# A two-layer decoder trunk on one core: three pairs of projection slabs of the sparse mixer as seven block products, and a new order of its begin

## The chip, the core and the metric

The kernel runs on one core of a Trainium2 chip. TensorE (PE in the profile, PEld for its weight loads) multiplies and writes to PSUM, which has eight banks; VectorE (DVE), ScalarE (ACT) and GpSimd (POOL) do the elementwise work, and transfers are issued from SyncE's queue (SP) and from ACT's. Each engine works through its own list of instructions in order and waits at semaphores for the others. The metric is the device time of one execution in microseconds (us).

## What is computed

A trunk of two layers over 512 tokens of width 1024, in float32. Each layer is a half-weighted SwiGLU network, a token mixer and a second half-weighted SwiGLU network, each behind an RMS norm. Layer 0 mixes with latent attention, layer 1 with native sparse attention. The change lies in the begin of the latter:

```python
def nsa_mixer(h, rel_bias, w_in, pos_k, w1_k, w2_k, pos_v, w1_v, w2_v, w_o):
    ...
    q, k_c, v_c, k_s, v_s, k_w, v_w, g = jnp.split(h @ w_in, cuts, axis=-1)
    ...
    gates = jax.nn.sigmoid(g.astype(jnp.float32)).astype(h.dtype).reshape(B, S, G, R, 3)
    ...
    kc = compress_blocks(k_c, blk_idx, pos_k, w1_k, w2_k)
    vc = compress_blocks(v_c, blk_idx, pos_v, w1_v, w2_v)
    ...
    o = gates[..., 0:1] * o_cmp + gates[..., 1:2] * o_sel + gates[..., 2:3] * o_win
    return o.reshape(B, S, H * NSA_V) @ w_o
```

Here h is the normed input (512 x 1024), q holds 16 heads of 64, and every k and v holds 4 groups of 64.

## The kernel before

**Numbers.** Every float32 factor is split in two parts of TensorE's faster format, high and low: ACT copies (rounding to the high part), DVE subtracts. A product is then three matmuls: high x high, high x low, low x high (`mm3`, L166 to L168, and `product`, L361 to L363). A weight slab is 128 columns of a projection, 1024 x 128, held as a tile of 128 x 1024; `wslab` loads it into one of two raw buffers (tile wr), and ACT and DVE split it into one of three tiles w (L147, L149). While the attention runs, POOL does the subtraction instead (L153).

**Block products.** A network's gate and up slab are two outputs of the same input. Their two halves of the weights' rows and the two halves of the tokens make a 2 x 2 by 2 x 2 block product, which the kernel forms with seven products of 12 matmuls of 256 columns in place of eight (`ffn`, L492 to L504). For this it needs sums of blocks: of the input (`combine`, L236 to L244: tiles y, u, and the split into a tile four) and of the weights (`wsums`, L346 to L353: tile s1, sums in place in the two raw tiles, three splits of 128 x 1024 and one of 128 x 512). Results come out in tiles px, pq and pg in PSUM, with copies on ACT and two additions on DVE.

**The sparse mixer's begin** (`nsa`, L1078 to L1117) uses plain slabs, 24 matmuls of 512 columns each (`proj`, and `pieces` in quarters). In the program's order: two slabs of compression keys (`tokens`, PSUM tile pcm); the norm's factors (`norm_col`: sums pc by TensorE, a chain of twelve small DVE instructions on tile small; `norm_bcast`: tile pb, copied to row); their layout into xc (`layout`, DVE, 8 instructions); two slabs of compression values; the compression network (`hidden`, tile ph, 16 matmuls); the keys of group 0 (`keys(0)`, PSUM tile pp, then t and four parts); the layout of the values; `pkc`; the second `hidden`; two query slabs (`query(0)`, `query(1)`); the values and gates (tiles pvg, 96 matmuls of 304 columns; `values` then splits them in alternation on ACT and DVE, and ACT forms the sigmoid gat); and `pvc`. 

**The attention behind it** runs in tiles (`attend`): scores on TensorE (L1180, L1205), softmax on DVE, ACT and POOL, transposes and the product with the values on TensorE. Into it `make` hands pieces of later projections by tile numbers, in group 1 the keys of group 1 at tiles 11 to 19. 

**What sets the order.** The order of the instructions on each engine is set before the run by a scheduler that interleaves the program's parts by its own estimates; the program gives the tiles and their buffers. PSUM's banks go by tags: two of mm, two of S, three of T, one of o. `mm_bank` turns through the first three kinds; `bank` takes the one that is named. A tile whose buffers are all in use waits until the oldest is read.

Of the kernel before, what the change touches and what calls it, by code (L numbers as in the profile page):

```python
# [11 lines left out]
F32 = mybir.dt.float32  # L12
# [33 lines left out]
FGAINS = "a0", "b0", "a1", "b1"  # L46
LASTK = 4
# [17 lines left out]
class Kern:  # L65
# [13 lines left out]
    def setup(self):  # L79
        nc, cp, a = self.nc, self.cp, self.a  # L80

        self.nw, self.odd, self.nq = 0, 0, 0
        self.first = self.wp.tile([P, 2048 + 3 * PAD], F32R, tag="w0", name="w")
        small = self.wp.tile([P, 80], F32, name="small")
        self.vtc, self.small_sums, self.stc = small[:, :12], small[:, 12:16], small[:, 32:]
        self.sts, self.nst = [small[:, 12 + 4 * i : 16 + 4 * i] for i in range(5)], 0
        self.gains = cp.tile([P, 64], F32, name="gains")
        nc.scalar.dma_start(self.gains[:, :53], a["gains"])  # L90
        self.ident = cp.tile([P, P], F32, name="ident")
        nc.scalar.dma_start(self.ident, a["c_ident"])
# [7 lines left out]
        self.ngains = cp.tile([P, 32], F32, name="ngains")  # L100
        for i, x in enumerate(FGAINS):
# [125 lines left out]
    def combine(self, p):  # L227


        nc, fp = self.nc, self.fp  # L230
        y = fp.tile([P, 1024], F32, tag="fh", bufs=3, name="y")
        u = fp.tile([P, 1024 + 2 * PAD], F32, tag="fl", bufs=3, name="u")[:, :1024]
        for e in range(2):
            c = p + KP * e
            with self.tc.issue_after(self.weights.ins) if self.weights else nullcontext():
                nc.scalar.activation(y[:, e * S : e * S + S], self.h[c], AF.Copy, scale=self.gains[:, self.ng + c : self.ng + c + 1])  # L236
# [6 lines left out]
        t = self.four()  # L243
# [57 lines left out]
    def proj(self, src, m, xh, xl, name, w=None):  # L301
# [3 lines left out]
        p = self.mm_bank(name)  # L305
# [50 lines left out]
    def product(self, j, w, out, first, last):  # L356
        mm = self.nc.tensor.matmul
        wh, wl = w[j]
        for p in range(KP):
# [3 lines left out]
            mm(out, wl[:, p], xh, start=False, stop=last and p == KP - 1, skip_group_check=True)  # L363

# [566 lines left out]
    def nsa(self, gain_next):  # L931
        nc, tc, a = self.nc, self.tc, self.a
        with ExitStack() as cx:
# [13 lines left out]
            xh, xl = self.xh, self.xl  # L947
            kt = [self.four() for _ in range(2)]
            kp = self.parts(kt[0]) + self.parts(kt[1])
            pcp, self.qt = self.parts(self.four()), self.parts(self.four())  # L950
# [18 lines left out]
            def keys(g):  # L969
# [3 lines left out]
                def done(p):  # L973
                    tt.append(qp.tile([P, S], F32, tag="t", bufs=2, name="t"))
                    nc.vector.tensor_tensor(tt[0], p, row, op=ALU.mult)
# [11 lines left out]
                return pieces(a["nsa_w_k"][g], done, [partial(part, br) for br in range(2)])  # L987
# [29 lines left out]
            def query(t2):  # L1017
# [3 lines left out]
                def done(p):  # L1021
                    tt.append(qp.tile([P, S], F32, tag="t", bufs=2, name="t"))
                    nc.vector.scalar_tensor_tensor(tt[0], p, 0.125, row, op0=ALU.mult, op1=ALU.mult)
# [8 lines left out]
                return pieces(a["nsa_w_q"][t2], done, [partial(part, e) for e in range(2)])  # L1032
# [3 lines left out]
            with tc.tile_pool(name="cmp", bufs=1, reuse_waits="tile") as bp:  # L1036
# [5 lines left out]
                def tokens(kind):  # L1042
                    return [self.proj(a["nsa_w_c"][2 * kind + gp], P, xh, xl, "pcm") for gp in range(2)]

                def layout(kind, ps):
# [6 lines left out]
                    for gp, p in enumerate(ps):  # L1052
                        for e in range(2):
                            g = 2 * gp + e
                            for odd in range(2):
                                src, rs = [t[64 * e : 64 * e + 64, :].rearrange("p (n l o) -> p n l o", l=8, o=2)[:, :, :, odd] for t in (p, row)]
                                dst = xc[64 * odd : 64 * odd + 64, :, 32 * g : 32 * g + 32].rearrange("p l n -> p n l")
                                nc.vector.tensor_tensor(dst, src, rs, op=ALU.mult)
# [19 lines left out]
                ps = tokens(0)  # L1078
                col = self.norm_col(D, self.s2)
                nc.scalar.activation(row, self.norm_bcast(col), AF.Copy)  # L1080
# [4 lines left out]
                for f in kf[:3]:  # L1085
                    f()
                xc = layout(1, ps)
                pk = self.mm_bank("pkc")
                nc.tensor.matmul(pk[:, : G * 32], w2, hid.rearrange("p g n -> p (g n)"), start=True, stop=True)
                at = lambda t: t[:, 96:].rearrange("p (g n) -> p g n", g=G)[:, :, 0:32]  # L1090
                self.split(pk[:, : G * 32].rearrange("p (g n) -> p g n", g=G), at(kch), at(kcl))
                for f in kf[3:]:
                    f()
                hid, w2 = hidden(1, xc)
                for f in query(0) + query(1):
                    f()

                pv = [self.mm_bank("pvg") for _ in range(4)]
# [7 lines left out]

                pk = self.mm_bank("pvc")
# [6 lines left out]
                for j in range(4):  # L1114
                    values(0, j, pv[j])
                    nc.scalar.activation(gat[:, j, :], pv[j][:, 256:VG], AF.Sigmoid, scale=col[:, j : j + 1])
                nc.vector.tensor_tensor(gcmp, gat[:, :, 0 : 3 * H : 3], rvalid[:, :, None].to_broadcast([P, 4, H]), op=ALU.mult)  # L1117
# [319 lines left out]
```

## Time and profile before

| | |
|---|---|
| median of 3 runs (lowest, highest) | 1864.89 us (1862.98, 1866.41) |
| span of the profiled execution, first to last instruction | 1860.0 us |
| mean granted TensorE clock | 0.999 |
| the sparse mixer's begin (first pcm matmul to the first scores) | 1216.9 to 1280.0 us |

For the profiled execution only the span is given; the median of the runs stands 4.9 us above it. A row of a timeline shows start, duration, engine, line, operation, the tile written and the tiles read, and shapes. TensorE's matmuls overlap: their durations are modelled ends, so what a matmul takes of the engine is read from the distance between two starts.

### The profile page before, as it was taken

To read this page: it belongs to the slowest core of one execution; us is meant where nothing else is said; L and a number is where in the kernel's file an instruction comes from. 1 tells how busy PE (TensorE), PEld (TensorE's weight loads), DVE (VectorE), ACT (ScalarE), POOL (GpSimd) and SP (SyncE) were. 2 spreads that over 40 slices of the span, in tenths; PEclk is the share of its full clock that TensorE was granted. 3 is DMA by queue.
4 is the path that set the end of the run, shared out by engine and by line. 5 is a ranking of instruction groups with operands and counts; after the bars stand their busy time and mean duration, and the time that the engine had idled before them with its cause. 6 is when DMAs were issued, how large, how long until landed. Compare 5 with 4: busy or idle time off the path is not lost. (4 is left out here: it accounts for less than half of the span.)

```text
span 1860.0 us, 32734 instructions
## 1 busy us (share of the span) xinstructions
PE 1841.1 (99%) x12440; PEld 1679.9 (90%) x12440; DVE 1542.0 (83%) x2862; ACT 1083.9 (58%) x2044; POOL 232.9 (13%) x323
## 2 busy tenths in 40 slices
PE   8999999999999999999999999999999999999998
PEld 8999999888889999998999999888888889999997
DVE  8988886688789888887998888765988989988885
ACT  8545554479776554555654545435887866544554
POOL 0000000046500000000000000015666600000000
PEclk9999999999999999999999999999999999999999
DMA  6333333142342333323233332333221124333321
GB/s 245 130 103 102 103 97 115 49 106 72 94 134 94 103 105 112 112 88 115 91 116 110 103 107 87 96 100 97 63 74 63 44 104 131 107 103 106 102 80 67
DMA packets 77901, 187.44 MB, mean 101 GB/s; under 512 B 9632, under 2 KB 37664, under 8 KB 77744
## 3 DMA queue, kind: packets, MB, share of 16 engines
q1 hardware_dynamic: 74640, 180.32, 30.3%
q10 hardware_dynamic: 3104, 5.03, 0.8%
q8 instruction: 98, 1.61, 0.3%
q14 instruction: 59, 0.48, 0.1%
HBM read 178.17 MB, written 2.16 MB: 97 GB/s over the span
## 5 line engine op out<-in xcount | busy, mean ns | idle before, releaser
L167 PE MATMUL pd<-al,wd 128*128 128x512 f32 x576 | 224.1, 389 | 0.0
L168 PE MATMUL pd<-ah,wd 128*128 128x512 f32 x576 | 224.0, 389 | 0.0
L166 PE MATMUL pd<-ah,wd 128*128 128x512 f32 x576 | 224.0, 389 | 0.0
L361 PE MATMUL px<-four,wh 128*128 128x256 f32 x632 | 175.2, 277 | 0.5 <-ACT pg L493 0.5
L363 PE MATMUL px<-four,wl 128*128 128x256 f32 x632 | 174.5, 276 | 0.0
L362 PE MATMUL px<-four,wh 128*128 128x256 f32 x632 | 174.5, 276 | 0.0
L362 PE MATMUL pq<-four,wh 128*128 128x256 f32 x632 | 174.5, 276 | 0.0
L363 PE MATMUL pq<-four,wl 128*128 128x256 f32 x632 | 174.4, 276 | 0.0
L361 PE MATMUL pq<-four,wh 128*128 128x256 f32 x632 | 174.4, 276 | 0.0
L174 ACT ACTIVATE wd<-wdr 128x384 fp32r<-128x384 f32 x192 | 99.2, 519 | 101.5 <-issue 75.5
L175 DVE TENSOR_TENSOR wl<-s,wh 128x512 fp32r<-128x512 f32 x79 | 54.6, 691 | 121.0 <-ACT wh L174 120.9
L413 DVE SCALAR_TENSOR_TENSOR h<-pd,h 128x512 f32<-128x512 f32 x216 | 148.5, 688 | 6.1 <-PE pd L168 6.1
L174 ACT ACTIVATE wh<-s 128x512 fp32r<-128x512 f32 x79 | 49.8, 630 | 136.5 <-PE px L362 131.2
L168 PEld LDWEIGHTS pd<-ah,wd 128*128 128x128 f32 x576 | 108.2, 188 | 22.5
L166 PEld LDWEIGHTS pd<-ah,wd 128*128 128x128 f32 x576 | 108.1, 188 | 19.4
L167 PEld LDWEIGHTS pd<-al,wd 128*128 128x128 f32 x576 | 108.0, 188 | 19.5
L361 PEld LDWEIGHTS px<-four,wh 128*128 128x128 f32 x632 | 118.6, 188 | 1.6 <-ACT pg L493 1.3
L362 PEld LDWEIGHTS px<-four,wh 128*128 128x128 f32 x632 | 118.6, 188 | 0.0
L363 PEld LDWEIGHTS pq<-four,wl 128*128 128x128 f32 x632 | 118.6, 188 | 0.0
L363 PEld LDWEIGHTS px<-four,wl 128*128 128x128 f32 x632 | 118.6, 188 | 0.0
L362 PEld LDWEIGHTS pq<-four,wh 128*128 128x128 f32 x632 | 118.6, 188 | 0.0
L361 PEld LDWEIGHTS pq<-four,wh 128*128 128x128 f32 x632 | 118.6, 188 | 0.0
(367 smaller groups left out, 6037.5 us busy)
## 6 DMA issues: line engine op xcount, KB each, us to landing
wr<-in_w_gu SPq DMA_DIRECT2D x93, 512.0 KB, 3.2
ru<-in_w_gu SPq DMA_DIRECT2D x79, 512.0 KB, 4.2
wdr<-in_w_down SPq DMA_DIRECT2D x192, 192.0 KB, 2.5
wdr<-in_w_down SPq DMA_DIRECT2D x24, 256.0 KB, 2.9
wr<-in_mla_w_o SPq DMA_DIRECT2D x8, 512.0 KB, 3.5
wr<-in_nsa_w_q SPq DMA_DIRECT2D x8, 512.0 KB, 3.5
th<-btab_d SPq DMA_DIRECT2D x16, 256.0 KB, 3.3
wr<-in_nsa_w_o SPq DMA_DIRECT2D x8, 512.0 KB, 3.6
```

Source lines behind the costliest of these rows:

```text
L166: mm(out, wh, xh, start=first, stop=False)
L167: mm(out, wh, xl, start=False, stop=False)
L168: return mm(out, wl, xh, start=False, stop=last)
L174: nc.scalar.activation(hi, src, AF.Copy)
L175: (nc.gpsimd if pool else nc.vector).tensor_tensor(lo, src, f32v(hi), op=ALU.subtract)
L361: mm(out, wh[:, p], xh, start=first and p == 0, stop=False, skip_group_check=True)
L362: mm(out, wh[:, p], xl, start=False, stop=False, skip_group_check=True)
L363: mm(out, wl[:, p], xh, start=False, stop=last and p == KP - 1, skip_group_check=True)
L413: nc.vector.scalar_tensor_tensor(self.h[c], p, 0.5, self.h[c], op0=ALU.mult, op1=ALU.add)
```

## The change

Three pairs of slabs go from 2 x 24 matmuls of 512 columns to seven products of 256: the compression values (`nsa_w_c[2:4]`), the keys of groups 0 and 1 (`nsa_w_k[0:2]`) and the queries of the first two pairs of heads (`nsa_w_q[0:2]`). The keys of group 1 leave the attention for this. The block sums of the input are formed with the negated gain (a new entry in ngains), so some results come with the other sign, which the following multiplication by row takes back. The values and gates move forward, behind the first pair, which stays plain.

```diff
+    def combos(self, p, y, u, t, gains, at):
+        ...
+                nc.scalar.activation(y[:, e * S : e * S + S], self.h[c], AF.Copy, scale=gains[:, at + c : at + c + 1])
...
+    def seven(self, w, uq, t):
+
+        nc = self.nc
+        x, q, g = self.bank("S", "px")[:, :HS], self.bank("mm", "pq")[:, :HS], self.bank("T", "pg")
+        self.product(1, w, x, True, False)
+        nc.scalar.activation(g[:, :HS], x, AF.Copy)
+        self.product(7, w, q, True, False)
+        nc.scalar.activation(uq[:, :HS], q, AF.Copy)
+        self.product(6, w, x, False, False)
+        nc.scalar.activation(uq[:, HS:], x, AF.Copy)
+        self.product(2, w, g[:, :HS], False, True)
+        self.product(5, w, x, False, True)
+        nc.scalar.activation(g[:, HS:], x, AF.Copy)
+        nc.vector.tensor_tensor(t[:, HS:], x, uq[:, :HS], op=ALU.add)
+        self.product(4, w, q, False, True)
+        nc.vector.tensor_tensor(t[:, :HS], q, uq[:, HS:], op=ALU.add)
+        self.product(3, w, g[:, HS:], False, True)
+        return g
...
-                def tokens(kind):
-                    return [self.proj(a["nsa_w_c"][2 * kind + gp], P, xh, xl, "pcm") for gp in range(2)]
+                def both(src):
+
+                    rg, ru = [self.wp.tile([P, 1024], F32, tag="wr", bufs=2, name="wr") for _ in range(2)]
+                    nc.sync.dma_start(rg, src[0])
+                    nc.sync.dma_start(ru, src[1])
+                    ...
+                    w[1], w[2] = split(rg)
+                    nc.vector.tensor_tensor(s1, u0, u1, op=ALU.add)
+                    nc.vector.tensor_tensor(u0, u0, g0, op=ALU.add)
+                    w[7], w[4] = split(ru)
+                    nc.vector.tensor_tensor(g0, g0, s1, op=ALU.add)
+                    nc.vector.tensor_tensor(g1, g1, g0, op=ALU.add)
+                    w[6], w[3] = split(rg)
+                    w[5], = split(s1)
+                    return self.seven(w, uq, t), t
...
-                    ph = self.mm_bank("ph")
+                    ph = self.bank("o", "ph")
...
+                ps = [self.proj(a["nsa_w_c"][gp], P, xh, xl, "pcm", tag="T") for gp in range(2)]
                 col = self.norm_col(D, self.s2)
                 nc.scalar.activation(row, self.norm_bcast(col), AF.Copy)
-                xc = layout(0, ps)
-                ps = tokens(1)
-                hid, w2 = hidden(0, xc)
-                kf = keys(0)
...
-                for f in query(0) + query(1):
-                    f()
...
+                for p in range(KP):
+                    yu = bp.tile([P, 16, P], F32, tag="w1", bufs=2, name="yu").rearrange("p l m -> p (l m)")
+                    self.combos(p, yu[:, :1024], yu[:, 1024:], sums[p], self.ngains, 8 * NGAINS.index("m1"))
+
+                pv = [self.bank(t, "pvg") for t in ("S", "mm", "S", "mm")]
...
+                for j in range(4):
+                    values(0, j, pv[j])
+                    nc.scalar.activation(gat[:, j, :], pv[j][:, 256:VG], AF.Sigmoid, scale=col[:, j : j + 1])
+                nc.vector.tensor_tensor(gcmp, gat[:, :, 0 : 3 * H : 3], rvalid[:, :, None].to_broadcast([P, 4, H]), op=ALU.mult)
+                xc = layout(0, ps)
+                ps = both(a["nsa_w_c"][2:4])
+                hid, w2 = hidden(0, xc)
+                xc = layout(1, ps)
+                ps = both(a["nsa_w_k"][0:2])
+                pk = self.bank("o", "pkc")
...
+                hid, w2 = hidden(1, xc)
+                ps = both(a["nsa_w_q"][0:2])
...
             def make(g, q, k, q2, c):
                 at(g, query(2 * g), *q)
-                at(g, keys(g), *k)
+                if g > 1:
+                    at(g, keys(g), *k)
```

Both raw tiles of a pair sit in wr, whose two buffers they fill; the three splits of 128 x 1024 take all three tiles w.

On DVE, the norm's chain of small instructions (from `small<-pc` on) stands before the change almost alone, with one split of a weight slab in it:

```order
L264 TENSOR_SCALAR small<-pc 128x4
L267 TENSOR_SCALAR small<-small 128x4
L268 TENSOR_SCALAR small<-small 128x4
L276 SCALAR_TENSOR_TENSOR small<-small 128x4
L277 TENSOR_TENSOR small<-small 128x4
L278 SCALAR_TENSOR_TENSOR small<-small 128x4
L149 TENSOR_TENSOR w<-wr,w 128x1024
L276 SCALAR_TENSOR_TENSOR small<-small 128x4
```

Now the block sums of the input (yu, sums) and the splits stand between its links; these rows are the second half of the chain, whose last link is L282:

```order
L282 SCALAR_TENSOR_TENSOR small<-small 128x4
L150 TENSOR_TENSOR w<-wr,w 128x608
L280 SCALAR_TENSOR_TENSOR small<-small 128x4
L247 TENSOR_TENSOR yu<-yu 128x256
L281 TENSOR_TENSOR small<-small 128x4
L176 TENSOR_TENSOR sums<-yu,sums 128x1024
L282 SCALAR_TENSOR_TENSOR small<-small 128x4
L176 TENSOR_TENSOR sums<-yu,sums 128x1024
L280 SCALAR_TENSOR_TENSOR small<-small 128x4
L1105 COPY xc<-pos 128x8x2
```

Behind it, still on DVE, the compression keys' layout (L1115) and the split of the values (v) share the place before the weights of product 7 (`w<-wr,w`):

```order
L1115 TENSOR_TENSOR xc<-pcm,row 64x32x8 x4
L179 SCALAR_TENSOR_TENSOR v<-pvg,small,v 128x2x64
L1115 TENSOR_TENSOR xc<-pcm,row 64x32x8
L179 SCALAR_TENSOR_TENSOR v<-pvg,small,v 128x2x64 x4
L1115 TENSOR_TENSOR xc<-pcm,row 64x32x8 x3
L176 TENSOR_TENSOR w<-wr,w 128x1024
```

Before, the split of the values followed the queries' work, with no layout in it:

```order
L1029 TENSOR_TENSOR q<-t,q 64x512
L1029 TENSOR_TENSOR four<-t,four 64x512
L178 SCALAR_TENSOR_TENSOR v<-pvg,small,v 128x2x64 x5
L175 TENSOR_TENSOR vc<-pvc,vc 128x64
L178 SCALAR_TENSOR_TENSOR v<-pvg,small,v 128x2x64 x3
```

On ACT, behind the gates of the last quarter, the copies out of the products (uq, pg) now stand in one line with the high parts of the next pair's weights (w):

```order
L1156 ACTIVATE gat<-pvg,small 128x48
L376 ACTIVATE uq<-pq 128x256
L175 ACTIVATE w<-wr 128x1024
L378 ACTIVATE uq<-px 128x256
L381 ACTIVATE pg<-px 128x256
L175 ACTIVATE ws<-s_14585 128x512
L175 ACTIVATE w<-wr 128x1024
```

So a copy that a product waits for comes behind a split that waits for a transfer.

More of the change, by code (lines that the diff above doesn't have):

```diff
@@ L947, in nsa @@
             xh, xl = self.xh, self.xl
+            sums = [self.four() for _ in range(2)]
             kt = [self.four() for _ in range(2)]
             kp = self.parts(kt[0]) + self.parts(kt[1])
-            pcp, self.qt = self.parts(self.four()), self.parts(self.four())
             def pieces(src, done, more, nk=4):
@@ L971, in keys, with done @@
                 tt = []
[L973 removed]
+                def done(p, sign=1.0):
                     tt.append(qp.tile([P, S], F32, tag="t", bufs=2, name="t"))
[L975 removed]
+                    if sign < 0:
+                        nc.vector.scalar_tensor_tensor(tt[0], p, sign, row, op0=ALU.mult, op1=ALU.mult)
+                    else:
+                        nc.vector.tensor_tensor(tt[0], p, row, op=ALU.mult)
                 def part(br):
@@ L985, in part @@
                     ks.setdefault(g, []).append((k1, k2))
-                return pieces(a["nsa_w_k"][g], done, [partial(part, br) for br in range(2)])
+                parts = [partial(part, br) for br in range(2)]
+                return [done] + parts if g < 2 else pieces(a["nsa_w_k"][g], done, parts)
             def values(gp, j, p):
@@ L1030, in part @@
                     qs.append(q)
-                return pieces(a["nsa_w_q"][t2], done, [partial(part, e) for e in range(2)])
+                parts = [partial(part, e) for e in range(2)]
+                return [done] + parts if t2 < 2 else pieces(a["nsa_w_q"][t2], done, parts)
             ks, vs, qs, pc, th, bank, pts = {}, {}, [], {}, {}, {}, {}
@@ L1076, in hidden @@
                     return hid, w2
-                ps = tokens(0)
+                ps = [self.proj(a["nsa_w_c"][gp], P, xh, xl, "pcm", tag="T") for gp in range(2)]
                 col = self.norm_col(D, self.s2)
                 nc.scalar.activation(row, self.norm_bcast(col), AF.Copy)
-                xc = layout(0, ps)
-                ps = tokens(1)
-                hid, w2 = hidden(0, xc)
-                kf = keys(0)
-                for f in kf[:3]:
-                    f()
[L1087 to L1094, printed above, removed]
-                for f in query(0) + query(1):
-                    f()
-                pv = [self.mm_bank("pvg") for _ in range(4)]
+                for c in range(KC):
+                    for e in range(2):
+                        self.xc["LR"[e], c] = [t[:, e * HS : e * HS + HS] for t in (xh[c], xl[c])]
+                sums += [bp.tile([P, 4 * S], F32R, tag="sums", bufs=2, name="sums") for _ in range(2)]
+                for p in range(KP):
+                    yu = bp.tile([P, 16, P], F32, tag="w1", bufs=2, name="yu").rearrange("p l m -> p (l m)")
+                    self.combos(p, yu[:, :1024], yu[:, 1024:], sums[p], self.ngains, 8 * NGAINS.index("m1"))
+                pv = [self.bank(t, "pvg") for t in ("S", "mm", "S", "mm")]
                 for k0 in range(0, KC, 3):
@@ L1105, in nsa @@
                             self.mm3(pv[j][:, :VG], xh[k0 + k][:, js], xl[k0 + k][:, js], wh[:, k], wl[:, k], k0 + k == 0, k0 + k == KC - 1)
-                pk = self.mm_bank("pvc")
+                for j in range(4):
[8 more added lines that the diff above has]
+                pk = self.bank("o", "pkc")
+                nc.tensor.matmul(pk[:, : G * 32], w2, hid.rearrange("p g n -> p (g n)"), start=True, stop=True)
+                at = lambda t: t[:, 96:].rearrange("p (g n) -> p g n", g=G)[:, :, 0:32]
+                self.split(pk[:, : G * 32].rearrange("p (g n) -> p g n", g=G), at(kch), at(kcl))
+                for g, p in enumerate(ps):
+                    f = keys(g)
+                    f[0](p, 1.0 - 2.0 * g)
+                    for x in f[1:]:
+                        x()
+                hid, w2 = hidden(1, xc)
+                ps = both(a["nsa_w_q"][0:2])
+                pcp, self.qt = self.parts(self.four()), self.parts(self.four())
+                for g, p in enumerate(ps):
+                    f = query(g)
+                    f[0](p, 1.0 - 2.0 * g)
+                    for x in f[1:]:
+                        x()
+                pk = self.bank("o", "pvc")
                 nc.tensor.matmul(pk[:, :DV], hid.rearrange("p g n -> p (g n)"), w2[:, :DV], start=True, stop=True)
```

40 lines of the change are left out of this document (26 added, 14 removed).

## The prediction

> **What bounds the kernel now.** First the page's busy times, then a table by windows for the two stretches that the change touches (the begin, 1217 to 1282 us; the attention where the keys of group 1 stood, 1290 to 1350), then the waits of TensorE's weight loads in the begin.
>
> ```profile
> PE 1841.1 (99%) x12440; PEld 1679.9 (90%) x12440; DVE 1542.0 (83%) x2862; ACT 1083.9 (58%) x2044; POOL 232.9 (13%) x323
> 1217.00:1282.00 65.00, 64.72 (x363) 56.62 (x362) 32.76 (x63) 23.02 (x38) 10.59 (x29) 1.00 0.34 105
> 1290.00:1350.00 60.00, 58.96 (x327) 47.79 (x326) 56.88 (x181) 54.40 (x144) 41.72 (x56) 1.00 0.22 71
> PEld pkc L1089 <- issue: 0.6, 1, 0.6
> ```
>
> The columns of the windows are length, then busy time of PE, PEld, DVE, ACT and POOL. TensorE is the bound everywhere; in the begin VectorE is free half of the time (32.8 of 65 us), in the attention it is at 95% and ACT at 91%. The largest wait of TensorE in the begin is 0.6 us. So fewer matmuls shorten the time as long as the other engines keep ahead, and the begin is where VectorE has room. The question is whether that room is enough.
>
> **TensorE: what is removed.** Starts of plain matmuls (512 columns), of block products (256) and of the values (304); each pair of rows is the first and the last of an unbroken run:
>
> ```profile
> 1216.89 0.39 PE L166 MATMUL pcm<-x,w 128*128 128x512 f32 x1
> ...
> 1221.88 0.39 PE L167 MATMUL pcm<-x,w 128*128 128x512 f32 x1
> ```
>
> ```profile
> 700.95 0.28 PE L361 MATMUL px<-x,w 128*128 128x256 f32 x1
> ...
> 704.93 0.28 PE L363 MATMUL px<-four,wl 128*128 128x256 f32 x1
> ```
>
> ```profile
> 1265.02 0.30 PE L166 MATMUL pvg<-w,x 128*128 128x304 f32 x1
> ...
> 1270.88 0.31 PE L166 MATMUL pvg<-w,x 128*128 128x304 f32 x1
> 1240.76 3.74 PE L1067 MATMUL ph<-xc,w 128*128 128x129 f32 x32
> 1244.25 0.47 PE L166 MATMUL pp<-x,w 128*128 128x512 f32 x1
> L298 PE MATMUL pb<-ident,small 128*128 128x128 f32 x8 | 1.1, 284 | 0.0
> ```
>
> 22 steps in 4.99 us are 0.227 each; 35 in 3.98 are 0.1137; 42 in 5.86 are 0.1395; a compression network takes 1244.25 - 1240.76 = 3.5. A pair costs 48 x 0.227 = 10.9 before and 84 x 0.1137 = 9.55 now; three pairs give back **4.0 us**. A term per matmul would eat into this, since 252 replace 144, but the rows show half the columns at half the time. [...]
>
> **VectorE: what is added.** Its groups in the networks, where the same sums are formed today, and in the begin:
>
> ```profile
> L175 DVE TENSOR_TENSOR w<-wr,w 128x1024 fp32r<-128x1024 f32 x38 | 46.3, 1219 | 0.0
> L347 DVE TENSOR_TENSOR s<-ru 128x512 f32<-128x512 f32 x39 | 26.7, 685 | 0.0
> L501 DVE TENSOR_TENSOR tu<-px,uq 128x256 f32<-128x256 f32 x40 | 16.7, 418 | 0.0
> L240 DVE TENSOR_TENSOR u<-y 128x512 f32<-128x512 f32 x4 | 2.8, 690 | 0.0
> L241 DVE TENSOR_TENSOR u<-y,u 128x256 f32<-128x256 f32 x5 | 2.1, 421 | 0.0
> ```
>
> ```profile
> L1058 DVE TENSOR_TENSOR xc<-pcm,row 64x256 f32<-64x256 f32 x16 | 10.0, 625 | 2.2 <-ACT row L1080 1.9
> L178 DVE SCALAR_TENSOR_TENSOR v<-pvg,small,v 128x128 fp32r<-128x128 f32 x8 | 2.5, 348 | 10.2 <-ACT v L177 10.2
> L149 DVE TENSOR_TENSOR w<-wr,w 128x608 fp32r<-128x608 f32 x1 | 0.8, 792 | 0.1
> L983 DVE TENSOR_TENSOR four<-t,four 64x512 fp32r<-64x512 f32 x2 | 1.4, 686 | 0.0
> 1228.58 0.48 PE L166 MATMUL pcm<-x,w 128*128 128x512 f32 x1
> 1228.76 0.16 DVE L264 TENSOR_SCALAR small<-pc 128x4 f32<-128x4 f32 x1 [1.41 <-PE pc L285]
> ```
>
> The input's sums: four times 0.69 + 2 x 0.42 + 1.22 = 11 us. A pair of weights: three splits of 1.22, one of 0.69, four sums of 0.69, two additions of 0.42, 7.95 against 2 x 1.22, so 5.5 more, 16.5 for three. The keys of group 1 bring 5 x 0.69 and a split that POOL did before, 4.7. VectorE's 32.8 us become **65 us**. TensorE's begin becomes 65 - 4 + 5.4 (the moved slab, 24 x 0.227) = 66. So the engine with half its time free turns into one as full as TensorE, in an order fixed beforehand, with ACT between its steps. I therefore walk the queues as they now stand, each wait being what TensorE reaches too early. ACT's rows, a load's landing, and POOL's half of a slab:
>
> ```profile
> L147 ACT ACTIVATE w<-wr 128x1024 fp32r<-128x1024 f32 x8 | 8.5, 1064 | 24.6 <-PE pcm L168 13.6 <-PE pvg L168 4.0 <-PE pp L168 4.0
> L177 ACT ACTIVATE v<-pvg,small 128x128 fp32r<-128x128 f32 x8 | 2.6, 372 | 0.5 <-PE pvg L168 0.3 <-DVE v L178 0.2
> L1116 ACT ACT_TABLE_LOAD x1 | 1.3, 1283 | 0.0
> L1116 ACT ACTIVATE gat<-pvg,small 128x48 f32<-128x48 f32 x4 | 1.2, 308 | 0.4 <-DVE v L178 0.4
> L1028 ACT ACTIVATE four<-t 64x512 fp32r<-64x512 f32 x4 | 2.5, 624 | 0.0
> wr<-in_nsa_w_k SPq DMA_DIRECT2D x2, 512.0 KB, 3.4
> L153 POOL TENSOR_TENSOR w<-wr,w 128x512 fp32r<-128x512 f32 x30 | 39.6, 1340 | 51.6 <-ACT w L147 51.3
> ```
>
> 1. *The norm's chain.* From pc to its last link VectorE now has 12 small steps of about 0.17 (2.0), 2 x 0.69 + 4 x 0.42 of sums, a split of 0.79, three of 1.22, 0.18 and 0.69: 10.4 us. TensorE, which goes on 0.2 earlier (1228.58 against 1228.76), reaches pb after 67 matmuls of the values, 9.35. It waits **1.2**.
> 2. *The values' banks.* px takes a bank of pvg and waits for its gat. VectorE from pb on: 0.18 + 3 x 0.69, four layouts of 0.625, one v of 0.35 = 5.1; then ACT's and VectorE's v in turn, 1.35; then ACT's table load and gat, 1.6: 8.0. TensorE has pb's 1.1 and 29 x 0.1395 = 5.15. It waits **2.9**.
> 3. *First pair.* Two v and three layouts (2.5) and the split for product 7 (1.22) end 10.05 after pb; TensorE, at 8.05, is there after 14 matmuls, 9.65: 0.4. Product 6 needs a sum, three v, and ACT's 1.06: 0.6. Behind the sigmoid and a waiting split a copy comes late: 0.3. Together **1.3**.
> 4. *Second pair.* After product 5, VectorE has two additions, a sum, eight layouts and a split, 0.84 + 0.69 + 5.0 + 1.22 = 7.75, begun 0.5 late behind a load; TensorE has product 3 and half of 4, the network's 3.5 and product 1, about 6.5: 1.7. Then posb 0.15, 3 x 0.69 and ACT's 1.06 against 1.8 of products: 1.5. With late copies 0.5: **3.7**.
> 5. *Third pair.* From product 3 of the second pair to product 6's low weights: 1.25 late, two t, kc 0.3, eight parts of 0.69, 1.22, two sums, vc 0.2, ACT 1.06, 1.22: about 14. TensorE has 9.9 to do (pkc 0.5, four products 5.5, the network 3.5, 0.4 of others): 4.1. POOL's low part of the next slab, the copies behind ACT's splits and the query parts before the scores add 1.5: **5.6**.
>
> Sum 14.7. The 0.6 us that TensorE waits there today goes into it. The edits without a term: the combos' ACT work (eight copies, four splits) lies under 48 + 36 matmuls, and its end is in term 1; the two loads of the compression network are issued behind the last split of term 1, some 18 us ahead of its first use, and land in 8.5 (last row below); POOL's memsets stand ahead of all.
>
> [...]
>
> **The attention** loses 5.4 us of TensorE's filler and, on VectorE, 5 x 0.69 = 3.4. If TensorE sets its pace all 5.4 are gained (which the sum above already counts, as the slab is only moved); if VectorE does, 3.4 x 60/56.9 = 3.6. Less work on ACT and POOL could give a little more than 5.4. Loss -1 to 1.8; I take **1.0**, nearer VectorE's 95%.
>
> **Sum.** 14.7 - 0.6 - 4.0 + 1.0 = 11.1 on the span of 1860.0, so 1871.1; the median stands 4.9 above the span: **1876.0 us**. The terms' ends: I allow a third of 14.7 for steps that queue otherwise, and the attention's 2: 1869 to 1883. Loads of a pair that land late cost more. Their lower bound is nothing, their upper one the slowest load of the stretch:
>
> ```profile
> w<-in_nsa_w SPq DMA_DIRECT2D x2, 0.5 KB, 8.5
> ```
>
> That is 5 us over a usual landing, for two pairs 10.
>
> **Rivals.**
> - *VectorE keeps ahead* (faster). If the order leaves splits and chains early enough, TensorE waits no more than today, the attention gives its full 5.4, and the change its 4: 1861. Its place is pb and the first px, with VectorE ahead there and staying so; it decides where all new waits stay under 1 us; the networks, where the same pair runs without waits, speak for it, but there the next pair's raw slabs have further buffers and no layouts, keys or values stand between. 8%.
> - *About no change.* Waits of 1 to 7.3 us, up to half the walk: terms 1 and 2 hold, the pairs hide the rest. 1865. 14%.
> - *Forecast*, 1869 to 1883: 62%.
> - *Loads bind.* Each pair fills both raw buffers; its successor's load starts only when its own splits are read, and ACT's queue stands behind that load. With landings as of the last row it costs up to 10 more: 1886. Against it: in the order, the next high part is asked for after two products. 16%.
> - *The change doesn't do what it says*: no sign, 144 matmuls of 512 go and 252 of 256 come.
>
> Faster by over 0.2% (about what a measurement of this kernel can tell, 3.7 us): 0.08; within: 0.14; slower: 0.62 + 0.16 = 0.78. The range 1864 to 1887 leaves out the faster case, half of the unchanged one and the worst loads.
>
> **What would show it.** Right: TensorE idle for a microsecond before pb and three before the first px, released by ACT's gat; waits in products 7 and 6 of each pair released by VectorE's w; VectorE above 9 tenths in the begin; the attention about 4 to 5 us shorter. Wrong: px starting with pvg's end, idle time in the attention instead of the begin, or px waiting for loads.

## The result, and the profile after

| | before | after |
|---|---|---|
| median of 5 runs (lowest, highest), us | 1863.79 (1862.53, 1866.41) | 1878.51 (1876.26, 1879.23) |
| ratio to before, 95% interval | | 1.0073 [1.0061, 1.0086] |
| span of the profiled execution, us | 1860.0 | 1874.5 |
| first scores of the sparse mixer, us from the start | 1280.0 | 1299.3 |

Slower, by 14.7 us; 1876.0 was predicted. The rows below are those of the profiled execution, which took 1876.26 us, the least of the five. The busy times of the changed kernel's page:

```profile
PE 1844.1 (98%) x12548; PEld 1684.5 (90%) x12548; DVE 1566.4 (84%) x2904; ACT 1102.2 (59%) x2074; POOL 235.2 (13%) x321
```

Its windows in the begin, up to where the scores run (columns: length, then busy time of PE, PEld, DVE, ACT and POOL with their instructions, granted clock, DMA share, GB/s):

```profile
1227.00:1247.00 20.00, 17.61 (x122) 17.02 (x121) 19.83 (x45) 13.46 (x23) 0.00 (x0) 0.96 0.57 166
1247.00:1262.00 15.00, 14.99 (x122) 14.71 (x122) 11.43 (x20) 7.04 (x12) 0.00 (x0) 0.94 0.23 71
1262.00:1282.00 20.00, 17.19 (x139) 16.16 (x137) 16.44 (x27) 11.37 (x21) 0.00 (x0) 1.00 0.15 53
1282.00:1302.00 20.00, 14.52 (x84) 11.65 (x85) 8.80 (x13) 7.71 (x12) 14.08 (x22) 1.00 0.56 157
```

VectorE is full from 1227 to 1247 (19.83 of 20 us) and less and less so behind that, while TensorE loses most in the last of the four windows, where VectorE is busy for 8.80 us only. So an average over the begin would mislead: at its start VectorE may be the bound, at its end it is something else. The waits of TensorE's weight loads from 1217 to 1305 us (engine, tile and line, what was waited for: us in total, times, longest) name them:

```profile
PEld pp L169 <- POOL w L154: 3.6, 1, 3.6
PEld px L365 <- ACT gat L1156: 2.6, 1, 2.6
PEld sc L1202 <- DVE four L1056: 2.5, 3, 1.2
PEld pq L367 <- DVE w L176: 1.4, 2, 0.9
PEld px L365 <- ACT w L175: 1.2, 1, 1.2
PEld pg L365 <- ACT pg L374: 1.1, 1, 1.1
PEld pq L365 <- ACT uq L376: 0.7, 1, 0.7
PEld px L367 <- DVE w L176: 0.5, 1, 0.5
PEld sc L1202 <- DVE q L1056: 0.4, 1, 0.4
PEld px L365 <- ACT uq L378: 0.4, 2, 0.2
PEld pb L302 <- issue: 0.2, 1, 0.2
```

They add up to 14.6 us: 4.8 end with an instruction of VectorE, 6.0 with one of ACT, 3.6 with POOL's and 0.2 with none that the profile shows. Before, the begin had 1.3 (0.6 before pkc and 0.7 in two others). The largest was not expected in this size. On POOL's timeline it reads:

```profile
1282.94 7.01 POOL L1186 TENSOR_SCALAR vcm<-vc 32x128 fp32r<-32x128 f32 x16 [58.07 <-DVE vc L176]
1290.03 2.52 POOL L154 TENSOR_TENSOR w<-wr,w 128x512 fp32r<-128x512 f32 x2
```

and before the change:

```profile
1271.44 2.53 POOL L153 TENSOR_TENSOR w<-wr,w 128x512 fp32r<-128x512 f32 x2 [48.26 <-ACT w L147]
1276.48 2.53 POOL L153 TENSOR_TENSOR w<-wr,w 128x512 fp32r<-128x512 f32 x2 [2.51 <-ACT w L147]
1280.52 5.64 POOL L1113 TENSOR_SCALAR vcm<-vc 32x128 fp32r<-32x128 f32 x16 [1.51 <-DVE vc L175]
```

The low halves of the next query slab stood in front of the 16 copies into vcm; now they stand behind them, because pvc no longer ends the begin. The third pp matmul waits for such a half, and product 5 of the queries, their sums and the scores are queued behind that matmul.

A second loss is in no row of waits. Behind the stop before the first px, TensorE ran at half clock (windows of one microsecond; the number before the last two is the granted clock):

```profile
1245.00:1246.00 1.00, 0.34 (x1) 0.34 (x2) 0.97 (x3) 0.99 (x5) 0.00 (x0) 0.68 0.00 0
1246.00:1247.00 1.00, 1.00 (x6) 1.00 (x6) 0.99 (x2) 0.32 (x2) 0.00 (x0) 0.50 0.00 0
1247.00:1248.00 1.00, 1.00 (x7) 1.00 (x7) 0.97 (x3) 0.00 (x0) 0.00 (x0) 0.50 0.00 0
1248.00:1249.00 1.00, 1.00 (x7) 1.00 (x7) 0.76 (x2) 0.37 (x2) 0.00 (x0) 0.62 0.41 102
```

Taking the clock as 1 or 0.5, the two mixed windows put it at half from 1245.36 to 1248.76, 3.4 us; 0.3 of them TensorE stood anyway, so this costs (3.4 - 0.3) / 2 = 1.5 us, an estimate that takes TensorE's pace to go with the clock: the matmuls of 256 columns start 0.21 us apart there and 0.12 behind it.

For the attention, the last matmul of its projection, before and after:

```profile
1513.41 0.40 PE L168 MATMUL po<-ohl,w 128*128 128x512 f32 x1
```

```profile
1526.87 0.40 PE L169 MATMUL po<-ohl,w 128*128 128x512 f32 x1
```

From the first scores to there it takes 233.4 us before and 227.6 after, 5.8 less. But 20 matmuls of the next query slab now run ahead of the first scores, where 6 did (14 x 0.227 = 3.2), and 5.4 us of the keys have left: 8.6 less to do, so 2.8 are lost, of which 1.7 are the waits of the later scores in the table above. What is left, 1.1, is the attention's own loss.

**The account of the span's 14.5 us:** waits 14.6 - 1.3 = 13.3, half clock 1.5, the attention 1.1, TensorE's saving -4.0, together 11.9. Behind the attention 1.0 more is lost (13.5 of the 14.5 are there by the last po). About 1.6 stays without a row: by distances of starts the stops before the first px and before pp are 2.5 and 3.3 us longer than a usual step, no more than their rows of 2.6 and 3.6.

### The profile page after: what moved, and what is told of

It reads as the page before. It is cut to its first block, busy times and chain, and to the rows that moved or that the text cites. A ratio compares the mean times of both kernels' runs of the same rounds, so it can differ in the third digit from the quotient of the medians.

```text
span 1874.5 us, 33019 instructions
## 1 busy us (share of the span) xinstructions
PE 1844.1 (98%) x12548; PEld 1684.5 (90%) x12548; DVE 1566.4 (84%) x2904; ACT 1102.2 (59%) x2074; POOL 235.2 (13%) x321
```

## The experiments

Each is compared with the kernel before on its own chip, by the ratio; "excess" is that ratio less one, times 1864 us. The changed kernel's excess is 13.6 us, 11.4 to 16.0. Line numbers in a run's rows are those of its own kernel, a few off the changed kernel's.

| run | ratio, 95% interval | excess, us |
|---|---|---|
| e1_low_on_vector | 1.0065 [1.0049, 1.0082] | 12.1 |
| e2_layout_late | 1.0063 [1.0048, 1.0078] | 11.7 |
| f4_both_mends | 1.0062 [1.0050, 1.0075] | 11.6 |
| e3_free_bank | 1.0087 [1.0072, 1.0102] | 16.2 |
| e4_order_alone | 1.0011 [1.0002, 1.0020] | 2.1 |
| f2_moved_keys | 1.0006 [0.9998, 1.0015] | 1.1 |
| e6_queries_plain | 1.0044 [1.0029, 1.0059] | 8.2 |
| e7_values_plain | 1.0056 [1.0041, 1.0071] | 10.4 |
| f1_keys_alone | 1.0024 [1.0014, 1.0033] | 4.5 |
| e8_own_raw | 1.0078 [1.0061, 1.0095] | 14.5 |
| e9_low_on_pool | 1.0119 [1.0104, 1.0134] | 22.2 |
| f3_values_between | 1.0051 [1.0039, 1.0064] | 9.5 |

### Order or products

The new order with plain slabs; the loop of combos left out, no changed signs:

```diff
                 def both(src):
+                    return [self.proj(src[i], P, xh, xl, "pcm") for i in range(2)]
...
-                for p in range(KP):
-                    yu = bp.tile([P, 16, P], F32, tag="w1", bufs=2, name="yu").rearrange("p l m -> p (l m)")
-                    self.combos(p, yu[:, :1024], yu[:, 1024:], sums[p], self.ngains, 8 * NGAINS.index("m1"))
```

> The new order with plain slabs: the three pairs are two slabs of 24 matmuls of 512 columns each again, the input's block sums are not formed; values and gates stay forward, the keys of group 1 stay in the begin. Theory (the block products' own work makes the waits): TensorE has 4.0 us more to do than in the changed kernel, VectorE about 28 us less; the waits in the pairs go (about 5 us), the wait before the first slab behind pvg goes, what stays is at the end (POOL's low part, the query parts: up to 5 us): 1866 us, between 1863 and 1869. Rival (the order makes them: nothing is left to cover the end once the values are forward): the waits at the end stay or grow and the time is 1872 or more.

1866.34 us: as the theory had it. The block products with their sums carry 13.6 - 2.1 = 11.5 us, the order and the moved keys 2.1 (0.4 to 3.7). In the same 85 us TensorE is busy for 82.67 and VectorE for 49.74 (in the changed kernel 74.32 and 62.40):

```profile
1217.00:1302.00 85.00, 82.67 (x443) 71.05 (x442) 49.74 (x92) 32.82 (x57) 22.48 (x48) 1.00 0.38 117
```

Then the moved keys by themselves, in the kernel before:

```diff
-                for f in kf[3:]:
+                for f in kf[3:] + keys(1):
                     f()
...
-                at(g, keys(g), *k)
+                if g > 1:
+                    at(g, keys(g), *k)
```

> The kernel before, in its own order with plain slabs, with the keys of group 1 moved out of the attention into its begin, behind those of group 0. Theory (the 2.0 us of the run with the new order and plain slabs come from the values standing forward, so that nothing covers the query parts; the moved keys pay for themselves): within 1 us of before, 1863.5 to 1865.5. Rival (the attention gives back less than the 5.4 us that it loses, the prediction's term of 1.0): 1865 to 1866.5, and the values forward cost about nothing.

1864.85 beside 1864.19 us: no difference that can be told. The interval, -0.4 to 2.8 us, says that the attention gives back about half or more of the 5.4 us that it loses; the prediction's loss of 1.0 lies inside it. How the 2.1 us divide between the moved keys and the values' place these two runs can't say.

### Pair by pair

The queries plain (the values likewise, with `nsa_w_c[2:4]`, and without the sign in `layout`), then both:

```diff
-                ps = both(a["nsa_w_q"][0:2])
+                ps = [self.proj(a["nsa_w_q"][g], P, xh, xl, "pp") for g in range(2)]
...
                 for g, p in enumerate(ps):
                     f = query(g)
-                    f[0](p, 1.0 - 2.0 * g)
+                    f[0](p, 1.0)
```

> The third pair (queries) goes back to two slabs of 24 matmuls of 512 columns; the first two pairs stay block products. Theory (each pair brings its own waits by its steps between VectorE and ACT): TensorE has 1.33 us more to do, the waits that the third pair holds in the changed kernel (uq 0.7, low weights of product 6 0.5, pp behind POOL 3.6, of which the run with VectorE's low part showed 2.8 to count, scores behind the query parts 2 of 2.9) go: 4 to 6 us off, 1873.5 us. Rival (VectorE's queue is full from 1228 to 1265 and that alone is late): the third pair costs what its 5.5 us of VectorE work cost at most where VectorE is free a third of the time (5.0 of 10 us in 1282 to 1292), so under 2 us off, 1877.

> The first pair (compression values) goes back to plain slabs; keys and queries stay block products. Theory (the bank of pvg): the stop before px (2.5 us) and the slow clock behind it (1.5) go, 1.33 of TensorE comes back, the second pair keeps its waits (2.2): about 3 us off, 1875.5 us. Rival (VectorE's queue is what is late in 1228 to 1265): 5.5 us less stand in it there, so the second pair's waits go too: 5 us or more off, 1873.5 us or less.

> In the new order only the second pair (keys of groups 0 and 1) is a block product; compression values and queries are plain slabs. The input's block sums (11 us of VectorE) stay. Theory (the waits hang on what stands in VectorE's and ACT's lists beside the products, so pairs do not add up): between the run with all slabs plain (1866.3) and the one with two pairs (1872.1 without the third): TensorE 1.33 us less than all plain, the second pair's own waits 2 to 4 us, 1867 to 1870. Rival (each pair has its own fixed price): third 6.4 and first 4.1 taken from 1878.5 leave 1868 as well, so this run tells only by its waits: under the theory the wait before px and the slow clock go with the values, under the rival the second pair keeps the 2.2 us that it has in the changed kernel.

Without the third pair the excess falls by 5.4, without the first by 3.2, without both by 9.1, though each takes 1.33 us of TensorE's saving with it. The second pair with the input's sums costs 4.5 - 2.1 = 2.4. By these numbers the prices add (8.6 against 9.1), as the rival of the last run says, but that can't be leaned on. Each excess has an interval of two to three microseconds to either side. The waits in the begin do not add: they are 14.6 in the changed kernel, 7.7 without the third pair, 8.4 without the first and 4.9 without both (each up to the scores), so 13.1 taken singly against 9.7 together. And the clock came in between: in the profiled executions TensorE ran at half clock for 3.4 us in the changed kernel and without the third pair, not at all with the keys alone, and for three stretches of 3.4 without the first pair (its profiled execution was the slowest of four, 1875.44 us, that of the keys alone the second fastest of ten, 1867.37):

```profile
1263.62:1267.03 3.41, 3.41 (x18) 3.41 (x17) 1.38 (x2) 0.39 (x1) 0.00 (x0) 0.50 0.36 135
1280.69:1284.10 3.41, 3.41 (x18) 3.41 (x18) 1.14 (x1) 0.74 (x2) 0.00 (x0) 0.50 0.29 71
1294.34:1297.75 3.41, 3.23 (x8) 2.02 (x8) 3.03 (x4) 0.36 (x2) 1.01 (x2) 0.50 0.67 238
```

Half of TensorE's busy time in them, 5.0 us, is the loss by the same estimate, where the changed kernel's is 1.5. So the waits that went with the first pair came to 6.2 us, and part of that was lost to the clock; 1874.41 lies between the two forecasts of that run. Whether the prices of the pairs add stays open. In the run without the third pair POOL's wait is gone from the table and the scores' waits are 1.2 and 1.0 in place of 2.5 and 0.4; product 6 of the second pair keeps its 1.2. With the keys alone one wait of 2.4 is left of the products, and its chain can be read in two timelines, ACT's

```profile
1259.78 1.28 ACT L1130 ACT_TABLE_LOAD   x1
1262.67 0.36 ACT L1130 ACTIVATE hid<-ph,posb 128x124 f32<-128x124 f32 x1 [1.61 <-DVE posb L1126]
1262.94 0.38 ACT L374 ACTIVATE pg<-px 128x256 f32<-128x256 f32 x1
```

and VectorE's:

```profile
1258.62 2.57 DVE L1115 TENSOR_TENSOR xc<-pcm,row 64x256 f32<-64x256 f32 x4
1261.22 1.23 DVE L176 TENSOR_TENSOR w<-wr,w 128x1024 fp32r<-128x1024 f32 x1
1262.48 0.16 DVE L1126 COPY posb<-ph 128x1 f32<-128x1 f32 x1
```

Product 6 needs the bank that ACT's copy pg reads; the copy stands behind hid, hid waits for posb, and posb, a column of 0.16 us, stands behind a layout and a split. So a pair's wait can come from the network beside it.

### The two waits of most weight

The low part on VectorE, for the one slab:

```diff
                 def load():
+                    pool, self.lo_pool = self.lo_pool, self.lo_pool and not dve
                     w.extend(self.wslab(src, (KC, P)))
+                    self.lo_pool = pool
```

> The low part of the first query slab behind the three pairs is formed by VectorE instead of POOL; nothing else. Theory (places in queues): POOL's halves stand behind its 16 copies vcm, which run to 1290.0; ACT's high part is there at 1287.4 and VectorE is free, so pp's third matmul comes near 1288.7 instead of 1291.35, the last products, the query parts and the scores move up with it: 2 to 2.7 us off, 1876 us beside 1878.5 of the changed kernel. Rival (loads bind): the next slabs' high parts wait for transfers (1.4 to 2.6 us in ACT's rows), so the scores come no earlier and the gain is under 0.7 us. Rival (VectorE is the bound of the begin as a whole): no gain, the wait comes back at the scores.

The wait for POOL is gone, but the scores' waits for the query parts grow from 2.5 to 3.4:

```profile
PEld sc L1204 <- DVE four L1058: 3.4, 3, 2.1
```

The first scores start at 1295.95 in place of 1299.28 (the second row is the changed kernel's):

```profile
1295.95 0.50 PE L1204 MATMUL sc<-four,kc 128*128 128x512 f32 x1 [1.64 <-DVE four L1058]
```

```profile
1299.28 0.50 PE L1202 MATMUL sc<-four,kc 128*128 128x512 f32 x1 [0.69 <-DVE four L1056]
```

The span is 2.2 us shorter, the median 1875.68. By the ratio the gain (1.5 us) is within the intervals; that the wait went and part of it came back at the scores is what the trace shows.

The layout queued behind the first pair's weights (`six` is the split for product 6), then with a free bank as well:

```diff
-                xc = layout(0, ps)
+                pcm = ps
                 ps = both(a["nsa_w_c"][2:4])
+                with tc.issue_after(self.six.ins):
+                    xc = layout(0, pcm)
```

```diff
-                pv = [self.bank(t, "pvg") for t in ("S", "mm", "S", "mm")]
+                pv = [self.bank(t, "pvg") for t in ("mm", "o", "mm", "S")]
```

> The layout of the compression keys (eight instructions, 5.0 us of VectorE) is queued behind the split for product 6 of the first pair; banks as in the changed kernel. Theory (places in queues): the wait before the first px stays near 2.5 us, since ACT's table load and gat now stand behind seven v and end near 1245.9 whoever is ahead on VectorE; the waits in products 7, 6 and 5 of the first pair (0.4 us) go, the layout may make the network late by up to 1 us: total within 1 us of 1878.5. Rival (term 2 as predicted: VectorE's layouts in front of v hold the bank): the wait before px falls by 1.5 us or more, the clock stays up, and the time falls by 2 us or more, to 1876.5 or less.

> As the run with the late layout, and the four banks of the values are named so that one bank of S is free: px no longer waits for a bank of pvg. Theory (the bank): px starts with the end of pvg, the 2.5 us and the slow clock behind it (15 matmuls at 0.21 in place of 0.114 us, 1.4 us) go; pb stands nine matmuls earlier in TensorE's list and waits up to 1.3 us: 2 to 4 us off the changed kernel, 1874.5 to 1876.5. Rival (VectorE is the bound): px starts early, but the splits for products 7 and 6 come no earlier, TensorE waits there instead, and the time stays within 1 us of the run with the late layout.

With the layout late the wait before px stays:

```profile
PEld px L365 <- ACT gat L1157: 2.5, 1, 2.5
```

On ACT's timeline of that run:

```profile
1244.57 1.42 ACT L178 ACTIVATE v<-pvg,small 128x128 fp32r<-128x128 f32 x5 [0.47 <-PE pvg L169]
1246.00 1.28 ACT L1157 ACT_TABLE_LOAD   x1
1247.30 0.69 ACT L1157 ACTIVATE gat<-pvg,small 128x48 f32<-128x48 f32 x3
```

So VectorE's layouts are not what holds the bank; ACT's v, which wait for the last matmuls of pvg, and the table load behind them do. The time, 1876.06 us, is one that the rival allowed, but by the ratio it can't be told from the changed kernel, and the rival's reason is not there: the wait before px is the same, while the wait before pp is 1.1 in place of 3.6. With a bank free, px starts at once, and the time is no better (1880.45 us):

```profile
PEld pq L365 <- ACT w L175: 3.7, 1, 3.7
PEld pp L169 <- POOL w L154: 3.5, 1, 3.5
```

```profile
1227.00:1262.00 35.00, 31.50 (x245) 30.72 (x243) 32.70 (x67) 18.80 (x34) 0.00 (x0) 1.00 0.41 125
```

TensorE runs through the first pair and meets VectorE's list in the second, where ACT's high part waits for a sum of VectorE that now stands behind both layouts; VectorE is busy for 32.70 of 35 us. In this stretch VectorE's work as a whole is late, and a wait removed comes back: that is the rival's mechanism. Its time (within 1 us of the run with the late layout) is missed by 4.4 us, and a part of that is the clock: half clock for 10.2 us, 6.8 of them behind the stop of 3.7 and 3.4 behind the one of 3.5, a loss of 4.8 us by TensorE's busy time in them, where the late layout had 3.4 us of half clock and lost 1.7.

Both mends at once:

> The changed kernel with the two mends that helped by themselves: the first query slab's low part on VectorE (2.8 us) and the layout queued behind the first pair's weights (2.4 us). Theory (separate places): they add, 1873.3 us. Rival (one queue behind both; what one saves the other finds gone): 1875 to 1876.

1875.64 us, where the rival put it and no better than each alone. The wait for POOL is gone, but the scores wait 4.3 for the query parts. By the ratio (9.3 to 14.0) a sum of the two gains, 13.6 - 1.5 - 1.9 = 10.2, is not excluded.

### Loads

```diff
-                    rg, ru = [self.wp.tile([P, 1024], F32, tag="wr", bufs=2, name="wr") for _ in range(2)]
+                    rg, ru = [bp.tile([P, 1024], F32, tag="rr", bufs=3, name="rr") for _ in range(2)]
```

> The pairs' raw weights get three buffers of their own in place of the two that all slabs share. Theory (loads bind): VectorE's waits for a transfer (1.00 and 1.03 us on the sums of the second and third pair) and ACT's (1.37, 1.56 and 2.58 us on the next slabs' high parts) go, and with the earlier start of each pair most of the 14 us of waits in the begin: 5 us or more off, 1873 us or less. Rival (queues of VectorE and POOL bind): the sums only move forward into VectorE's full stretch, the wait before px stays, POOL's low part stays behind its vcm copies: within 2 us of 1878.5.

1878.55 us, the rival's time, but the run does not isolate the loads. VectorE's waits of 1.00 and 1.03 us for a transfer fall to 0.35 and none, and with that the lists came out otherwise: pvc and POOL's copies stand at the end again, the waits before px for gat and before pp for POOL are gone, and others came (3.1 before the network, 2.9 for copies, 1.9 for weights, 3.5 at the scores; 12.2 in all), and half clock lasted 10.3 us. So the loads' part remains open. The prediction's rival of that name is answered by the changed kernel itself: in its begin no wait of TensorE ends with a transfer, and the pairs' sums wait for one by 1.0 us at most.

### Taking work from VectorE

```diff
-        self.split(u, t[:, :1024], t[:, 1024:])
+        self.split(u, t[:, :1024], t[:, 1024:], pool=gains is self.ngains)
...
-                    nc.vector.tensor_tensor(k2[es, :], t[es, :], f32v(k1[es, :]), op=ALU.subtract)
-                    nc.vector.tensor_tensor(k2[os, :], t[es, :], f32v(k1[es, :]), op=ALU.subtract)
+                    low = nc.gpsimd if g < 2 else nc.vector
+                    low.tensor_tensor(k2[es, :], t[es, :], f32v(k1[es, :]), op=ALU.subtract)
+                    low.tensor_tensor(k2[os, :], t[es, :], f32v(k1[es, :]), op=ALU.subtract)
```

> The low parts of the input's four block sums (4 x 1.22 us) and of the keys of groups 0 and 1 (8 x 0.69 us) are formed by POOL instead of VectorE, 10.4 us out of VectorE's queue; POOL is idle from 1225 to 1283 in the changed kernel. Theory (VectorE's queue is the bound of the begin): the norm's chain, the first pair's weights and the third pair's weights come 2 to 5 us earlier, and the time falls by 3 to 6 us, to 1872.5 to 1875.5. Rival (each wait is the place of one step: ACT's table load, the bank, POOL's vcm copies): the wait before px stays above 2 us, POOL's copies come later still, and the time is within 1.5 us of 1878.5.

1885.72 us, which neither theory gave. Two timelines of this run, VectorE's and POOL's:

```profile
1230.97 2.30 DVE L245 TENSOR_TENSOR yu<-yu 128x512 f32<-128x512 f32 x1 [0.44 <-ACT yu L241]
...
1235.99 2.30 DVE L280 SCALAR_TENSOR_TENSOR small<-small 128x4 f32<-128x4 f32 x1
```

```profile
1227.11 5.62 POOL L176 TENSOR_TENSOR four<-yu,four 128x1024 fp32r<-128x1024 f32 x2 [1.54 <-ACT four L175]
1235.72 2.55 POOL L176 TENSOR_TENSOR sums<-yu,sums 128x1024 fp32r<-128x1024 f32 x1 [3.00 <-ACT sums L175]
```

A sum that takes 0.69 us and a small step of 0.16 took 2.30 each while POOL's subtraction ran, and ended with it or just behind (at 1233.27 and 1238.29, the subtractions at 1232.73 and 1238.27). What held them up these rows do not show. The chain became later instead of earlier: TensorE waited 4.9 us before pb. Later it waited 6.6 before pp for POOL, and from 1217 to 1310 us it ran at half clock for 20.5. Since the edit brought these costs with it, the run decides nothing between the two theories.

### A kinder order

Two pairs (keys, queries), four plain slabs ahead of them, and the queries between two parts of the values:

```diff
+                p1 = [self.proj(a["nsa_w_c"][2 + i], P, xh, xl, "pcm", tag=t) for i, t in enumerate(("S", "mm"))]
+                p0 = ps
+                ps = both(a["nsa_w_k"][0:2])
+                with tc.issue_after(self.six.ins):
+                    xc = layout(0, p0)
+                hid, w2 = hidden(0, xc)
+                xc = layout(1, p1)
...
+                pv = [self.bank(t, "pvg") for t in ("T", "o", "mm", "S")]
                 for k0 in range(0, KC, 3):
                     nk = min(3, KC - k0)
+                    if k0 == 6:
+                        ps = both(a["nsa_w_q"][0:2])
```

> Two pairs (keys, queries) as block products in another order: four plain compression slabs, the keys' pair, both layouts queued behind its weights, the network, two thirds of values and gates, the queries' pair, the last third, with banks of their own for the values. TensorE has 2.67 us less than with plain slabs. Theory (the waits come from lists in which VectorE's work for a pair has no plain products beside it): with 22 us of plain products over the block sums and 10 us of values over the keys' parts and the queries' weights the waits in the begin fall under 3 us: 1861 to 1865, level with before or faster. Rival (VectorE's 56 us are too much for any order): waits of 5 us or more reappear in the network behind the layouts or before product 7 of the queries: 1868 or more.

1874.11 us, the rival's side. Both pairs run without a stop; the waits are elsewhere:

```profile
PEld pkc L1155 <- issue: 4.0, 1, 4.0
PEld sc L1206 <- DVE four L1056: 2.2, 3, 1.4
PEld pvg L168 <- DVE w L150: 1.8, 1, 1.8
PEld sc L1206 <- DVE q L1056: 1.4, 1, 1.4
```

```profile
1227.00:1267.00 40.00, 34.72 (x225) 31.75 (x224) 37.21 (x67) 23.48 (x33) 0.00 (x0) 0.97 0.41 121
```

VectorE is busy for 37.21 of 40 us. Sixteen layouts behind the keys' weights hold up the split of the values' weights (1.8) and posb, by which hid and then pkc come late (4.0), and pkc stands in TensorE's list ahead of values that could run. The clock falls to half twice, behind the stop before pkc and behind the waits at the scores, for 6.8 us together, a loss of 3.4. No kernel of this study is faster than the one before.

## Why the prediction was right or wrong

**The direction was right, the mechanism in part.** It said that VectorE would become as full as TensorE in the begin and that TensorE would wait inside the products, for the gates, and at the end; 1876.0 was forecast, 1878.5 measured. As a difference it was 11.1 against 14.7: the kernel before ran 1.1 us faster this time, which brought the two times nearer. That the block products make the loss is shown: all plain left 2.1 us. The sum of the terms, 14.7, met 14.6 of waits in the begin, but that is in good part luck, since the errors cancel: the first four terms came to 5.3 in place of 9.1, the fifth to 9.3 in place of 5.6. Term by term:

- Term 1, the chain before pb: 1.2 forecast, 0.2 found. The chain took 8.3 us, not 10.4, from the first of these rows to the end of the last. The prediction added up durations, but the rows overlap by some 0.08: a small step took about 0.1 of VectorE's time, not the 0.17 used (the second row starts 0.08 behind the first), and the sum of 0.68 behind it took 0.60.

```profile
1229.65 0.15 DVE L268 TENSOR_SCALAR small<-pc 128x4 f32<-128x4 f32 x1
1229.73 0.68 DVE L245 TENSOR_TENSOR yu<-yu 128x512 f32<-128x512 f32 x1
1230.33 0.16 DVE L271 TENSOR_SCALAR small<-small 128x4 int32<-128x4 int32 x1
...
1237.84 0.15 DVE L282 SCALAR_TENSOR_TENSOR small<-small 128x4 f32<-128x4 f32 x1
```

- Term 2, px behind the gates: 2.9 forecast, 2.6 found, released by ACT's gat as said. Its working put VectorE's layouts on the path; the run with the layout late has the same wait, so ACT's v and table load set it: the number nearly met, by another path. What it costs that ACT's and VectorE's v go in turn, 1.35 us in that working, no run shows; in the changed kernel ACT's v at 1242.95 waited 0.91 us for VectorE's.
- Term 3, first pair: 1.3 forecast, 0.2 found (a copy); no wait for weights. The half clock hid it: at full clock TensorE would have come to them 1.4 us sooner and waited about half a microsecond, an estimate from VectorE's rows (its split for product 7 ends at 1247.52, its sum for product 6 at 1248.76).
- Term 4, second pair: 3.7 forecast, 2.3 found (0.9 for low weights of product 7, 1.2 for high weights of product 6, 0.2 for a copy).
- Term 5, third pair and the scores: 5.6 forecast, 9.3 found. This is the term that was mis-sized most, and both of its halves were: 4.1 for weights that VectorE brings late behind the keys' parts was 1.0 (0.5 in product 7, 0.5 in product 6), and the 1.5 for POOL's low part, late copies and the query parts together was 8.3 (3.6 before pp, 1.1 and 0.7 for copies, 2.9 at the scores). It moved pvc forward without counting what that moves on POOL, the 7.0 us of vcm ahead of the slab's low half. The run with the low part on VectorE shows that the query parts are next late, by 0.9 of it.
- The half clock behind a stop, 1.5 us, was in no term.
- TensorE's saving of 4.0 can't be read alone in these runs; the counts are as said (12548 matmuls against 12440), and a changed spacing of the products was not looked for.
- The attention: 1.0 forecast, 1.1 found. "About 4 to 5 us shorter" was 5.8, since more of the next slab ran ahead of the scores.
- "VectorE above 9 tenths in the begin" holds from 1227 to 1247 only (19.83 of 20 us); from 1217 to 1302 it is 62.40 of 85, TensorE 74.32. And of the waits in "products 7 and 6 of each pair" the first pair has none.

**The rivals.** "VectorE keeps ahead" and "About no change" were wrong by the waits above; "Loads bind" by the changed kernel's own rows, not by the run with buffers of its own. Shown by the runs: that the products' own work makes 11.5 of the 13.6 us, that a free bank moves the wait into the second pair. Not shown: whether the prices of the pairs add, what the loads alone cost, and how the 1.6 us without a row and the 1.0 behind the attention come about.

## What to carry to other kernels

Fewer matmuls pay only where the engines that prepare them have room just there and just then (here 4.0 us were to be saved, and the begin's waits grew by 13.3): look at the stretch in windows, not at its mean, and count the work by the list in which it will stand. When a step is moved, follow what it releases on every queue: here sixteen small copies on POOL, released earlier, made a wait of 3.6 us, nearly the 4.0 that TensorE was to save; the run without that wait gave back 1.5 us by the ratio and 2.2 of the span. And a stop of TensorE of two to three microseconds can have a price beyond its length: behind the 2.6 us before px the clock was at half for 3.4 us, 1.5 us of loss, while it did not fall behind the 3.1 us before pp.

## What the runs showed of the hardware that was not expected

**The clock falls behind short stops, in steps of 3.4 us.** In the changed kernel and its variants half clock lasted 3.4 us or twice that: 6.8 us in the run with the free bank from 1262.4, where TensorE also stood for 3.7 us. It began behind stops of 2.5 and 2.6 us (before px), but in the changed kernel not behind the 3.1 us before pp at 1288 to 1291; in the run with the free bank it fell at 1293.2, behind the 3.5 us before pp, too. Counted off in stretches of 3.4 us from where the clock fell, TensorE was busy in the changed kernel for 0.40 of the stretch just before (in the runs with the low part on VectorE, the layout late and the queries plain 0.32, 0.33 and 0.31), while the stop before pp fell on two stretches, busy for 0.56 and 0.53. These shares are PE's busy time in windows of 3.41 us. No single share fits every case: in the run with the values between, the second fall, at 1295.0, came behind a stretch that was busy for 0.61, one of the run with POOL's low parts, at 1289.4, behind 0.59, and without the first pair one behind 0.48, while in the run with both mends a stretch of 0.49 had no fall behind it. What decides it is not settled here.

**VectorE's small steps.** A step on 128x4 shows 0.15 us and takes about 0.08 to 0.1 of the queue between independent instructions (in the changed kernel, from 1229.65 to 1229.73 and from 1230.33 to 1230.44); one that follows the step it depends on comes some 0.2 later (in the run with the free bank, at 1236.07, 1236.26 and 1236.46).

**VectorE beside POOL's subtraction.** In the run with POOL's low parts a sum and a small step of VectorE took 2.30 us in place of 0.69 and of 0.16, above.
